# Two-block transformer kernel: the odd layer's first projection with another order of its block products, later reads of PSUM and another order of its loads

## The chip, the cores and the metric

The kernel runs on one core of one Trainium2 chip. The metric is the time of one execution of the whole program on the device, in microseconds. The program has two blocks: a transformer block with gated linear attention, differential attention and a feed-forward part, and a second block of two layers. The change touches the last third of the second block alone, its odd layer.

## What is computed, as far as it matters here

The odd layer normalizes and modulates x (1024 tokens of 1024 channels) to h, multiplies h by `odd_w_in` (1024 x 3072), mixes the columns with a pooling and a short convolution, and multiplies by `odd_w_out`; the result is added to x.

```python
def odd_mixer(h, w_in, w_out, p_w, p_scale, conv_w):
    p = h @ w_in
    ...
    y_c = pool_mix(p[..., :o1], p_w, p_scale)
    c_gate, x_path, b_gate, z = p[..., o1:o2], p[..., o2:o3], p[..., o3:o4], p[..., o4:]
    y_d = b_gate * short_conv(c_gate * x_path, conv_w)
    y = jnp.concatenate([y_c, y_d], axis=-1) * jax.nn.silu(z)
    return y @ w_out
```

## The kernel before

**Precision.** Operands of a product are held as a high and a low part (`hi`, `lo`), and every product of a 128x128 weight block with 512 columns of activations is three matmuls: hi by hi, hi by lo, lo by hi. For weights ScalarE (ACT) copies the high part and GpSimd (POOL) subtracts for the low part; `split_part` does so for weights that come through the ring of the helper `pump` (`raw` tiles, loaded on SP's queue at L183).

**Seven products for eight.** The 24 column blocks of `odd_w_in` are taken in 12 pairs p (the table `ODD`). For a pair, the weights are four quarters a11, a12, a21, a22 (128 x 512 numbers each), and h is four quarters too: two halves of the channels, by tokens 0 to 511 and 512 to 1023. A scheme of Strassen and Winograd's makes the 2 x 2 block product out of 7 products m = 1 to 7, each of 4 blocks k, so 12 matmuls. The activation sides (`ops[m]`, "forms") are made once, in `differences`: m = 1 and 2 take the tokens 0 to 511 of h, which are there first; 5, 6, 7, 3 and 4 need the second half normalized (`normed`) and then sums and differences of both halves (t1, t2 and so on), each split into a high part on ACT and a low part. The weight sides (`ODD_W`) are quarters or the sums s1 to s4, formed on VectorE (DVE) by `quarter_sum` in place, split by `halves` in `weight_steps`. Six buffers hold the quarters; `quarter` loads one on SP's queue, `free` gives one back.

**Order.** `ODD_ORDER` lists the products (m, p). Pairs 0 and 1 were interleaved at the start, so that their products with the first half of h come first and the forms are made under them; from p = 2 on the order is 1, 6, 2, 7, 5, 4, 3. `weight_steps` gives each weight step a due time in products; `prepare(n + 3)` in the loop does what is due three products ahead.

**PSUM places.** A product fills one bank of 512 columns. Two products in a row share one tile of two banks (`halves` in `product`), a "place" here; three places are used in turn. `evac(p)` reads finished products in the order of the list `order[p]`: m = 1 is copied by ACT, the others are added by DVE to the running sums t0 (`v`) and t1 (`y`). Before the change it was called after every product:

```python
            if n > 1:
                evac(p)
            step()
```

`step` runs one piece of the work that follows a pair (`after`): for p < 4 the pooling, with two small products `ps_w` (L2000) in PE's queue, for p from 4 on the convolution and the gate.

**The end.** `odd_w_out` comes through `pump` again; x, which had been stored to HBM, is loaded back (`x<-x_d`, 4 MB in 4 transfers, L2074) before the last residual, whose first products are `ps_x` (L220). In the last pair the finished columns are split for that product (`y_split`), in pieces between the products. Almost all instructions are issued through one helper and show its line, L65 (L68 after the change); so they are told apart by the tiles' names.

## Time and profile before

| | |
|---|---|
| median of 3 runs | 2405.98 us (2405.83 to 2413.56) |
| the profiled execution's own time | 2409.9 us |
| its span in the trace | 2408.1 us, so 1.8 us lie around it |
| busy: PE / DVE / POOL / ACT | 91% / 67% / 45% / 36% |
| mean granted clock of TensorE | 0.962 of full speed |
| the odd layer's first projection, 84 products | about 1981 to 2308 us |
| what follows it (residual, final norm) | 2308 to 2408 us |

A row of the timeline has the start, the length, the engine and line, the operation with its output and inputs by name, a count, and in brackets the time that the engine stood idle before it with what ended that. Matmuls overlap, so their pitch is read from starts, not from lengths.

### The profile page before, as it was taken

How to read it: one execution, taken by the hardware profiler on the slowest of the kernel's cores; microseconds unless marked ns; L12 is line 12 of the kernel's file. 1: busy time of each engine (PE TensorE's matmuls, PEld its weight loads, DVE VectorE, ACT ScalarE, POOL GpSimd, SP SyncE). 2: the span in 40 equal slices, each digit the busy share in tenths (PEclk: the TensorE clock that was granted, in tenths of full speed). 3: DMA queues.
4: the chain of work that ended last, by engine and by line, in shares of the span. 5: the costliest groups of instructions: out<-in, count | busy, mean ns of one | idle time of the engine just before them, and what ended most of it. 6: DMA issues, size and time to landing. Idle time of an engine off the chain costs nothing. (4 is left out here: it accounts for less than half of the span.)

```text
span 2408.1 us, 28852 instructions
## 1 busy us (share of the span) xinstructions
PE 2181.5 (91%) x10024; PEld 1763.0 (73%) x10024; DVE 1618.0 (67%) x2642; ACT 861.4 (36%) x1432; POOL 1092.4 (45%) x843
## 2 busy tenths in 40 slices
PE   6999998899999999989999997988879985888888
PEld 3777777688878888878787875877767774666666
DVE  8665656688366866798777657689875567554534
ACT  4324331588443222222232344422224433222333
POOL 7333332498433322223556425555443536453543
PEclk8999899999999999999999999998989998999999
DMA  7355664985423445212333333654526531121143
GB/s 266 109 170 192 209 210 151 270 236 174 164 90 108 146 134 181 85 59 91 108 105 114 112 90 108 181 174 147 175 97 222 180 105 49 45 66 44 47 158 114
DMA packets 191402, 330.41 MB, mean 137 GB/s; under 512 B 47330, under 2 KB 88194, under 8 KB 190996
## 3 DMA queue, kind: packets, MB, share of 16 engines
q1 hardware_dynamic: 190960, 328.34, 42.3%
q8 instruction: 79, 1.29, 0.2%
q14 instruction: 71, 0.58, 0.1%
q10 hardware_dynamic: 292, 0.20, 0.0%
HBM read 264.90 MB, written 67.46 MB: 138 GB/s over the span
## 5 line engine op out<-in xcount | busy, mean ns | idle before, releaser
L65 POOL TENSOR_TENSOR lo<-raw,hi 128x512 fp32r<-128x512 f32 (+3 forms) x414 | 509.5, 1244 | 762.4 <-ACT hi L65 502.1
L65 ACT ACTIVATE hi<-raw 128x512 fp32r<-128x512 f32 (+3 forms) x418 | 217.9, 549 | 387.2 <-PE ps_g L220 143.1
L220 PE MATMUL ps_g<-h0hi,hi 128*128 128x512 f32 x552 | 222.4, 403 | 12.7 <-ACT h0hi L65 8.0
L220 PE MATMUL ps_g<-h0lo,hi 128*128 128x512 f32 x552 | 218.7, 396 | 5.7 <-POOL h0lo L65 5.7
L220 PE MATMUL ps_g<-h1lo,hi 128*128 128x512 f32 x552 | 216.6, 392 | 5.9 <-DVE h1lo L65 5.9
L220 PE MATMUL ps_g<-h0hi,lo 128*128 128x512 f32 x552 | 218.7, 396 | 1.9 <-DVE lo L65 1.4
L220 PE MATMUL ps_g<-h1hi,hi 128*128 128x512 f32 x552 | 220.4, 399 | 0.0
L220 PE MATMUL ps_g<-h1hi,lo 128*128 128x512 f32 x552 | 216.3, 392 | 0.0
L65 DVE SCALAR_TENSOR_TENSOR u<-ps_g,vecs,u 128x1023 f32<-128x1023 f32 (+3 forms) x94 | 114.1, 1214 | 92.5 <-ACT u L65 89.7
L65 POOL TENSOR_TENSOR lo<-a,hi 128x512 fp32r<-128x512 f32 x80 | 114.8, 1461 | 130.9 <-ACT hi L65 94.3
L220 PEld LDWEIGHTS ps_g<-h0hi,hi 128*128 128x128 f32 x552 | 105.4, 191 | 38.9 <-ACT h0hi L65 9.2
L220 PEld LDWEIGHTS ps_g<-h0lo,hi 128*128 128x128 f32 x552 | 105.4, 191 | 28.5 <-POOL h0lo L65 7.0
L220 PEld LDWEIGHTS ps_g<-h1lo,hi 128*128 128x128 f32 x552 | 104.6, 189 | 29.0 <-DVE h1lo L65 7.2
L220 PEld LDWEIGHTS ps_g<-h0hi,lo 128*128 128x128 f32 x552 | 105.5, 191 | 25.2 <-DVE lo L65 1.8
L1934 PE MATMUL ps_o<-t,hi 128*128 128x512 f32 x288 | 95.1, 412 | 31.6 <-ACT hi L65 18.7
L220 PEld LDWEIGHTS ps_g<-h1hi,hi 128*128 128x128 f32 x552 | 104.7, 190 | 24.4 <-issue 2.2
L220 PEld LDWEIGHTS ps_g<-h1hi,lo 128*128 128x128 f32 x552 | 104.5, 189 | 22.3
L220 PE MATMUL ps_d<-acthi,hi 128*128 128x512 f32 x272 | 109.4, 402 | 11.9 <-DVE u L65 8.9
L220 PE MATMUL ps_d<-actlo,hi 128*128 128x512 f32 x272 | 108.1, 397 | 0.0
L220 PE MATMUL ps_d<-acthi,lo 128*128 128x512 f32 x272 | 107.5, 395 | 0.0
L65 DVE TENSOR_TENSOR acc<-acc,sq 128x512 f32<-128x512 f32 x69 | 73.9, 1072 | 47.0 <-ACT sq L65 46.0
L65 ACT ACTIVATE hi<-a 128x512 fp32r<-128x512 f32 x80 | 45.7, 621 | 150.6 <-DVE a L65 148.3
(445 smaller groups left out, 5611.9 us busy)
## 6 DMA issues: line engine op xcount, KB each, us to landing
adw<-in_ada_w_dram SPq DMA_DIRECT2D x48, 512.0 KB, 3.5
raw<-in_w_up_dram SPq DMA_DIRECT2D x88, 256.0 KB, 3.0
adw<-in_w_ada_dram SPq DMA_DIRECT2D x32, 512.0 KB, 5.7
bias<-bias_d SPq DMA_DIRECT2D x32, 512.0 KB, 4.6
a<-in_odd_w_in_dram SPq DMA_DIRECT2D x60, 256.0 KB, 3.0
raw<-in_w_in_dram SPq DMA_DIRECT2D x50, 256.0 KB, 3.9
raw<-in_even_w_in_dram SPq DMA_DIRECT2D x44, 256.0 KB, 3.5
raw<-in_w_down_dram SPq DMA_DIRECT2D x72, 128.0 KB, 2.7
```

The costliest lines, as they stand in the source:

```text
L65: return f(*a, **k)
L220: self.PE.matmul(out, lhsT=a[:, k], rhs=b, start=first and n == 0, stop=last and n == 2)
L1934: PE.matmul(out, lhsT=a[:, k], rhs=b[k], start=k + n == 0, stop=k == 3 and n == 2)
```

## The change

Pair 0 is multiplied as eight plain block products, with weights that come whole through `pump` (columns 0 and 16 of `odd_w_in`; one more weight in `seq`), and two of its products accumulate into the bank of an earlier one: (3,0) on (5,0) and (4,0) on (6,0). So there are 85 products in place of 84. The order of the first 22 products is written out anew, and from p = 3 on it is 1, 2, 6, 7, 5, 4, 3. `evac` is called only when both products of a place are issued. All forms are split on VectorE instead of GpSimd, after all normalized quarters are made first. The weight sums s2 and s4 are formed right behind each other, and the quarter a12 is loaded earlier in the order. The reload of x is issued after the loop, so behind eight transfers of `odd_w_out`.

```diff
-ODD_ORDER = [(m, p) for m in (1, 2, 5, 6, 7, 3, 4) for p in range(2)] + [(m, p) for p in range(2, 12) for m in (1, 6, 2, 7, 5, 4, 3)]
+
+ODD_ORDER = [(1, 1), (2, 1), (1, 0), (8, 0), (2, 0), (9, 0), (5, 0), (6, 0), (5, 1), (3, 0), (4, 0), (3, 1), (6, 1), (7, 1),
+             (1, 2), (2, 2), (6, 2), (4, 1), (7, 2), (5, 2), (4, 2), (3, 2)]
+ODD_ORDER += [(m, p) for p in range(3, 12) for m in (1, 2, 6, 7, 5, 4, 3)]
...
-        self.seq += [(I["odd_w_in"][n], 8) for n in range(2)]
+        self.seq += [(I["odd_w_in"][n], 8) for n in (1, 0, 16)]
...
-                self.quarter_sum(p, "s1", "a21", "a22", "a22", ALU.add)
-                yield
-                self.quarter_sum(p, "s3", "a11", "a21", "a21")
-                yield
-                self.quarter_sum(p, "s2", "s1", "a11", "a11")
+            for out, x, y, place, op in (("s1", "a21", "a22", "a22", ALU.add), ("s3", "a11", "a21", "a21", ALU.subtract),
+                                         ("s2", "s1", "a11", "a11", ALU.subtract), ("s4", "a12", "s2", "a12", ALU.subtract)):
+                self.quarter_sum(1, out, x, y, place, op)
...
-        t12, t22, t1, t2 = [], [], [], []
+        t12 = [normed(place(7, 1, k, F32), k) for k in range(4)]
+        t22 = [normed(place(4, 1, k, F32), 4 + k) for k in range(4)]
+        yield
+        t1, t2 = self.temps, []
         for k in range(4):
-            t12.append(normed(place(7, 1, k, F32), k))
-            t1.append(temp())
             V.tensor_tensor(out=t1[k], in0=t12[k], in1=t11[k], op=ALU.subtract)
-            split(G, 5, t1[k], k)
+            split(V, 5, t1[k], k)
             yield
         for k in range(4):
-            t22.append(normed(place(4, 1, k, F32), 4 + k))
+            A.activation(out=ops[3][0][k], in_=t22[k], func=ACTF.Identity, bias=shift(k))
             t2.append(place(4, 0, k, F32))
             V.scalar_tensor_tensor(out=t2[k], in0=t22[k], scalar=shift(k), in1=t1[k], op0=ALU.add, op1=ALU.subtract)
-            split(G, 6, t2[k], k)
+            V.scalar_tensor_tensor(out=ops[3][1][k], in0=t22[k], scalar=shift(k), in1=f(ops[3][0][k]), op0=ALU.add, op1=ALU.subtract)
+            yield
+        for k in range(4):
+            split(V, 6, t2[k], k)
             yield
         for k in range(4):
             t = self.temps[k]
             V.scalar_tensor_tensor(out=t, in0=t22[k], scalar=self.dsh[:, k:k + 1], in1=t12[k], op0=ALU.add, op1=ALU.subtract)
-            split(G if k < 3 else V, 7, t, k)
+            split(V, 7, t, k)
             yield
-        for k in range(4):
-            A.activation(out=ops[3][0][k], in_=t22[k], func=ACTF.Identity, bias=shift(k))
-            V.scalar_tensor_tensor(out=ops[3][1][k], in0=t22[k], scalar=shift(k), in1=f(ops[3][0][k]), op0=ALU.add, op1=ALU.subtract)
         for k in range(4):
             t = self.temps[k]
             V.tensor_tensor(out=t, in0=f(ops[2][0][k]), in1=t2[k], op=ALU.subtract)
             V.tensor_tensor(out=t, in0=t, in1=f(ops[2][1][k]), op=ALU.add)
-            split(G, 4, t, k)
+            split(V, 4, t, k)
...
-            if m in (3, 4, 5, 7):
+            if m > 2:
                 self.free(p, ODD_W[m])
 
         def last(p):
             self.quarter_sum(p, "s4", "a12", "s2", "a12")
-            self.free(p, "s2")
-
-        for p in range(12):
+
+        for p in range(1, 12):
             at = lambda m: ODD_AT[m, p]
             for m in range(1 if p > 1 else 3, 8):
                 add(at(m), 0, halves, m, p)
@@ -1888,10 +1884,9 @@
                     add(at(1) - 3, 1, self.quarter, p, name)
                 add(at(1) + 0.1, 0, self.quarter_sum, p, "s1", "a21", "a22", "a22", ALU.add)
                 add(at(1) + 0.2, 0, self.quarter_sum, p, "s3", "a11", "a21", "a21")
-                add(at(6) - 0.5, 0, self.quarter_sum, p, "s2", "s1", "a11", "a11")
-            q = at(2) if p > 1 else at(7)
-            add(q - 2, 1, self.quarter, p, "a12")
-            add(q + 1, 0, last, p)
+                add(at(2) + 0.5, 0, self.quarter_sum, p, "s2", "s1", "a11", "a11")
+                add(at(2) - 2, 1, self.quarter, p, "a12")
+                add(at(2) + 0.6, 0, last, p)
...
-            if m == 2 and p < 2:
-                out = self.pst.tile([128, 512], F32, tag="t", name="ps_2")
+            again = p == 0 and m in (3, 4)
+            if again:
+                out = banks[m + 2, 0]
             elif halves:
...
-                if m < 3 and p < 2:
-                    self.product(self.odd0 + p, out, k + 4 * (m - 1), rh[k], rl[k], k == 0, k == 3)
+                if p == 0:
+                    self.product(self.odd0 + 1 + (m in (8, 9, 6, 4)), out, k + 4 * (m in (2, 9, 3, 4)), rh[k], rl[k],
+                                 k == 0 and not again, k == 3 and m not in (5, 6))
+                elif p == 1 and m < 3:
+                    self.product(self.odd0, out, k + 4 * (m - 1), rh[k], rl[k], k == 0, k == 3)
...
-                        while len(todo) > 1:
-                            step()
+                    while len(todo) > 1:
+                        step()
                     t0[p] = first(p)
-                    A.activation(out=t0[p][:, H[0]], in_=ps, func=ACTF.Copy)
+                if m in (1, 8):
+                    A.activation(out=(second(p) if m == 8 else t0[p])[:, H[1]], in_=ps, func=ACTF.Copy)
                     continue
                 u = [t[:, h] for t in (t0[p], second(p)) for h in H]
-                for out, x in {6: ((1, 0),), 2: ((0, 0),), 7: ((2, 1),), 5: ((3, 2), (1, 1)), 4: ((2, 2),), 3: ((1, 1),)}[m]:
+                how = {2: ((0, 1),), 6: ((1, 1),), 7: ((2, 1),), 5: ((3, 2), (1, 1)), 4: ((2, 2),), 3: ((1, 1),), 9: ((2, 3),)}
+                if p == 0:
+                    how[4] = (3, 3),
+                for out, x in how[m]:
...
+            if m == 4 and p == 0:
+                self.release(self.odd0 + 1)
+                self.release(self.odd0 + 2)
+            elif m == 2 and p == 1:
+                self.release(self.odd0)
+            elif p > 1 or p == 1 and m > 2:
...
-            prepare(n if n < 4 else n + 3)
+            prepare(n + (5 if p == 11 else 3))
...
-                evac(0)
-                evac(1)
-                self.temps = [t[:, h] for t in wide for h in H]
...
-            if n > 1:
-                evac(p)
+                self.temps = [t[:, h] for t in wide for h in H]
+            if not halves or (m, p) == (3, 11):
+                for q in range(max(p - 1, 0), p + 1):
+                    evac(q)
...
-                for a in range(2):
-                    for k in (0, 4):
-                        S.dma_start(out=self.x[:, k:k + 4, H[a]], in_=self.x_d[:, k:k + 4, H[a]])
             if not steps:
                 self.n_max = len(self.seq)
                 self.pump()
-        i = self.odd0 + 2
+        while todo:
+            step()
+        for a in range(2):
+            for k in (0, 4):
+                S.dma_start(out=self.x[:, k:k + 4, H[a]], in_=self.x_d[:, k:k + 4, H[a]])
+        i = self.odd0 + 3
```

**ACT, from the forms t7 to the last weight of pair 1.** `t70`, `t40` and `h1hi` are high parts of forms, `hi<-a...` those of weights; `a21_27663` holds the weight sum s3 of pair 1, for the product (7,1). Before:

```order
L65 ACTIVATE t70_28525<-y6_28491 128x512
L65 ACTIVATE t70_28530<-y6_28491 128x512
L65 ACTIVATE t70_28535<-y7_28492 128x512
L65 ACTIVATE t70_28540<-y7_28492 128x512
L65 ACTIVATE hi_28546<-a11_27673 128x512
L65 ACTIVATE h1hi_18152<-t41f_28449,m21_17426 128x512
L65 ACTIVATE h1hi_18152<-t41f_28457,m21_17426 128x512
L65 ACTIVATE h1hi_18152<-t41f_28465,m21_17426 128x512
L65 ACTIVATE h1hi_18152<-t41f_28473,m21_17426 128x512
L65 ACTIVATE t40_28575<-y6_28491 128x512
L65 ACTIVATE t40_28581<-y6_28491 128x512
L65 ACTIVATE t40_28587<-y7_28492 128x512
L65 ACTIVATE t40_28593<-y7_28492 128x512
L65 ACTIVATE hi_28597<-a21_27663 128x512
```

Now:

```order
L68 ACTIVATE t60_28576<-t40f_28530 128x512
L68 ACTIVATE t70_28593<-y6_28433 128x512
L68 ACTIVATE t70_28598<-y6_28433 128x512
L68 ACTIVATE hi_28602<-a12_27669 128x512
L68 ACTIVATE t70_28626<-y7_28434 128x512
L68 ACTIVATE t70_28631<-y7_28434 128x512
L68 ACTIVATE hi_28635<-a11_27667 128x512
L68 ACTIVATE t40_28653<-y6_28433 128x512
L68 ACTIVATE t40_28659<-y6_28433 128x512
L68 ACTIVATE t40_28677<-y7_28434 128x512
L68 ACTIVATE t40_28683<-y7_28434 128x512
L68 ACTIVATE hi_28687<-a21_27663 128x512
```

The weight for (7,1) stands behind the four forms t40 in both; the h1hi rows (form 3) have gone to an earlier place, and two weights stand between the forms.

**DVE, in the middle of the layer, one pair each.** `v` and `y` with a `ps_o` input are reads of products, `a` rows are weight sums. Before:

```order
L65 TENSOR_TENSOR y3_28496<-ps_o_29028,y3_28496 128x512
L65 TENSOR_TENSOR v_28974<-ps_o_29028,v_28974 128x512
L65 TENSOR_TENSOR a22_28987<-a21_28985,a22_28987 128x512
L65 TENSOR_TENSOR a21_28985<-a11_28983,a21_28985 128x512
L65 TENSOR_TENSOR a11_28983<-a22_28987,a11_28983 128x512
L65 TENSOR_TENSOR y3_28496<-ps_o_29075,y3_28496 128x512
L65 TENSOR_TENSOR v_28974<-ps_o_29075,v_28974 128x512
L65 TENSOR_TENSOR a12_29052<-a12_29052,a11_28983 128x512
```

Now:

```order
L68 TENSOR_TENSOR v_29287<-ps_o_29295,v_29287 128x512
L68 TENSOR_TENSOR y4_28439<-ps_o_29295,v_29287 128x512
L68 TENSOR_TENSOR a22_29273<-a21_29271,a22_29273 128x512
L68 TENSOR_TENSOR a21_29271<-a11_29269,a21_29271 128x512
L68 TENSOR_TENSOR y4_28439<-ps_o_29332,y4_28439 128x512
L68 TENSOR_TENSOR v_29287<-ps_o_29332,v_29287 128x512
L68 TENSOR_TENSOR y4_28439<-ps_o_29332,y4_28439 128x512
L68 TENSOR_TENSOR a11_29269<-a22_29273,a11_29269 128x512
L68 TENSOR_TENSOR a12_29312<-a12_29312,a11_29269 128x512
```

Before, the three sums of the next pair (s1, s3, s2) stood in front of a read of the next product's place; now s1 and s3 stand behind the reads of one whole place and s2 and s4 behind those of the next.

**SP, the end of the odd layer.** `a` rows are the last quarters of weights, `raw` rows transfers of `odd_w_out`. Before:

```order
L1723 DMA a12_30059<-in_odd_w_in_dram 128x512
L1723 DMA a22_30121<-in_odd_w_in_dram 128x512
L2074 DMA x_30213<-x_d_125 128x4x512 x4
L183 DMA raw_30218<-in_odd_w_out_dram 128x512
L183 DMA raw_30220<-in_odd_w_out_dram 128x512
L183 DMA raw_30222<-in_odd_w_out_dram 128x512
L183 DMA raw_30224<-in_odd_w_out_dram 128x512
```

Now:

```order
L1722 DMA a12_30024<-in_odd_w_in_dram 128x512
L1722 DMA a22_30104<-in_odd_w_in_dram 128x512
L186 DMA raw_30164<-in_odd_w_out_dram 128x512
L186 DMA raw_30166<-in_odd_w_out_dram 128x512
L186 DMA raw_30168<-in_odd_w_out_dram 128x512
L186 DMA raw_30170<-in_odd_w_out_dram 128x512
L186 DMA raw_30233<-in_odd_w_out_dram 128x512
L186 DMA raw_30235<-in_odd_w_out_dram 128x512
L186 DMA raw_30288<-in_odd_w_out_dram 128x512
L186 DMA raw_30290<-in_odd_w_out_dram 128x512
L2082 DMA x_30207<-x_d_125 128x4x512 x4
L186 DMA raw_30358<-in_odd_w_out_dram 128x512
```

The reload of x stood in front of all transfers of `odd_w_out`, and stands behind eight of them now.

## Rows read from the trace of the kernel before

**Rows 1.** Windows: length, busy PE, PEld, DVE, ACT, POOL (count), clock, DMA.
```profile
1980.00:2055.00 75.00, 47.72 (x177) 35.54 (x176) 53.55 (x55) 25.29 (x41) 44.14 (x33) 0.84 0.13 43
...
2020.00:2030.00 10.00, 1.92 (x5) 1.56 (x6) 9.86 (x10) 3.89 (x7) 8.20 (x6) 0.50 0.01 2
...
2055.00:2292.00 237.00, 203.37 (x843) 155.34 (x841) 123.25 (x154) 56.44 (x94) 110.80 (x79) 1.00 0.18 58
```
**Rows 2.** Timeline, PE, pairs 6 and 7: start, length, instruction, idle before and releaser.
```profile
2144.33 0.39 PE L1934 MATMUL ps_o<-h1lo,hi 128*128 128x512 f32 x1
...
2149.32 0.39 PE L1934 MATMUL ps_o<-t,lo 128*128 128x512 f32 x1
...
2151.24 0.47 PE L1934 MATMUL ps_o<-h1hi,hi 128*128 128x512 f32 x1 [1.53 <-ACT hi L65]
...
2198.44 0.47 PE L1934 MATMUL ps_o<-h1hi,hi 128*128 128x512 f32 x1 [1.53 <-ACT hi L65]
```
**Rows 3.** Timeline, DVE, at the gap that ends at 2151.24.
```profile
2148.23 2.26 DVE L65 TENSOR_TENSOR a<-a,a 128x512 f32<-128x512 f32 x3
2150.41 0.68 DVE L65 TENSOR_TENSOR y<-ps_o,y 128x512 f32<-128x512 f32 x1
```
**Rows 4.** Timeline, PE, the first 14 products: the long waits and the product after them.
```profile
1983.33 1.12 PE L405 MATMUL ps_r<-acc,ones 128*128 128x512 f32 x2 [1.55 <-DVE acc L65]
...
2028.08 1.19 PE L1934 MATMUL ps_o<-t,hi 128*128 128x512 f32 x2 [13.69 <-ACT hi L65]
...
2054.56 0.39 PE L1934 MATMUL ps_o<-h0hi,hi 128*128 128x512 f32 x1
```
**Rows 5.** Timeline, DVE, ACT and POOL, while the forms are made.
```profile
1985.87 0.75 DVE L65 SCALAR_TENSOR_TENSOR t71f<-x,s,rs 128x512 f32<-128x512 f32 x1 [2.53 <-ACT rs L65]
...
2000.19 1.78 DVE L65 SCALAR_TENSOR_TENSOR t41f<-x,s,rs 128x512 f32<-128x512 f32 x1
...
1999.68 3.43 POOL L65 TENSOR_TENSOR t<-t40f,t 128x512 fp32r<-128x512 f32 x2
...
2025.74 0.63 ACT L65 ACTIVATE t<-y 128x512 fp32r<-128x512 f32 x1 [0.70 <-DVE y L65]
2026.28 1.72 ACT L65 ACTIVATE hi<-a 128x512 fp32r<-128x512 f32 x3
```
**Rows 6.** Groups of instructions, 2055 to 2292: line, engine, shape, count, busy and mean ns, idle before.
```profile
L65 POOL TENSOR_TENSOR lo<-a,hi 128x512 fp32r<-128x512 f32 x68 | 97.5, 1460 | 116.7 <-ACT hi L65 80.1 <-PE ps_o L1934 26.0 <-issue 9.8
L65 ACT ACTIVATE hi<-a 128x512 fp32r<-128x512 f32 x66 | 37.3, 621 | 130.0 <-DVE a L65 130.0
L65 DVE TENSOR_TENSOR v<-ps_o,v 128x512 f32<-128x512 f32 x39 | 26.8, 688 | 52.6 <-PE ps_o L1934 49.2 <-ACT hi L65 3.4
L65 DVE TENSOR_TENSOR a<-a,a 128x512 f32<-128x512 f32 x37 | 25.4, 687 | 1.7
L2000 PE MATMUL ps_w<-y,pw 128*128 128x512 f32 x16 | 7.7, 603 | 2.6 <-DVE y L65 1.4 <-issue 1.2
L65 DVE SCALAR_TENSOR_TENSOR y<-y,v 128x1024 f32<-128x1024 f32 x4 | 6.9, 1714 | 0.1
```
**Rows 7.** Timeline, PE, ACT, SP and DVE, at the layer's end.
```profile
2303.59 0.77 PE L1934 MATMUL ps_o<-h1hi,hi 128*128 128x512 f32 x1 [11.86 <-DVE y L65]
...
2308.01 0.39 PE L220 MATMUL ps_x<-h0hi,hi 128*128 128x512 f32 x1
...
2298.59 1.27 ACT L65 ACTIVATE hi<-raw 128x512 fp32r<-128x512 f32 x2 [15.29 <-DMA raw<-in_odd_w_out_dram]
...
2284.86 2.52 SPq L2074 DMA_DIRECT2D x<-x_d  x4
2287.48 37.18 SPq L183 DMA_DIRECT2D raw<-in_odd_w_out_dram  x14
...
2317.73 0.75 DVE L65 SCALAR_TENSOR_TENSOR x<-ps_x,m,x 128x512 f32<-128x512 f32 x1 [4.92 <-PE ps_x L220]
```
**Rows 8.** The page's table of DMA issues: the loads of weight quarters.
```profile
a<-in_odd_w_in_dram SPq DMA_DIRECT2D x60, 256.0 KB, 3.0
```

More of the change, by code (lines that the diff above doesn't have):

```diff
@@ L1413, in second_block @@
             self.release(i)
-            self.n_max = self.odd0 + 2
+            self.n_max = self.odd0 + 3
             self.pump()
@@ L1680, in even_out @@
         self.dsh = tp.tile([128, 64], F32, name="dsh")[:, 0:4]
-        for p in range(2):
-            for name in ("a21", "a22", "a11"):
-                self.quarter(p, name)
+        for name in ("a21", "a22", "a11", "a12"):
+            self.quarter(1, name)
         ns = ExitStack()
@@ L1699, in first_sums @@
         def first_sums():
-            for p in range(2):
-                self.quarter_sum(p, "s1", "a21", "a22", "a22", ALU.add)
-                yield
-                self.quarter_sum(p, "s3", "a11", "a21", "a21")
-                yield
-                self.quarter_sum(p, "s2", "s1", "a11", "a11")
+            for out, x, y, place, op in (("s1", "a21", "a22", "a22", ALU.add), ("s3", "a11", "a21", "a21", ALU.subtract),
+                                         ("s2", "s1", "a11", "a11", ALU.subtract), ("s4", "a12", "s2", "a12", ALU.subtract)):
+                self.quarter_sum(1, out, x, y, place, op)
                 yield
@@ L1742, in differences @@
         yield
-        def temp():
-            return tmp.tile([128, 512], F32, tag="nm", name="nm")
         def split(eng, m, src, k):
@@ L1905, in odd_layer @@
         banks, halves, turn, t0, vs, todo, late = {}, [], [2], {}, {}, deque(), []
-        order = [[1, 6, 2, 7, 5, 3, 4] if p < 2 else [1, 6, 2, 7, 5, 4, 3] for p in range(12)]
+        order = [[1, 8, 2, 9, 3, 4], [1, 2, 6, 7, 5, 3, 4]] + [[1, 2, 6, 7, 5, 4, 3] for p in range(2, 12)]
         P = 8
@@ L1926, in product @@
             banks[m, p] = out
-            rh, rl = ops[m]
+            rh, rl = ops[{8: 1, 9: 2, 6: 5, 4: 3}.get(m, m) if p == 0 else m]
             for k in range(4):
-                if m < 3 and p < 2:
-                    self.product(self.odd0 + p, out, k + 4 * (m - 1), rh[k], rl[k], k == 0, k == 3)
+                if p == 0:
[3 more added lines that the diff above has]
+                    self.product(self.odd0, out, k + 4 * (m - 1), rh[k], rl[k], k == 0, k == 3)
                 else:
@@ L1935, in product @@
                 yield
-            if m == 2 and p < 2:
-                self.release(self.odd0 + p)
-            elif m > 2 or p > 1:
+            if m == 4 and p == 0:
[4 more added lines that the diff above has]
+            elif p > 1 or p == 1 and m > 2:
                 del self.odd_split[m, p]
@@ L1947, in evac @@
                 if m == 1:
-                    if p > 1:
-                        while len(todo) > 1:
-                            step()
+                    while len(todo) > 1:
+                        step()
                     t0[p] = first(p)
-                    A.activation(out=t0[p][:, H[0]], in_=ps, func=ACTF.Copy)
+                if m in (1, 8):
+                    A.activation(out=(second(p) if m == 8 else t0[p])[:, H[1]], in_=ps, func=ACTF.Copy)
                     continue
                 u = [t[:, h] for t in (t0[p], second(p)) for h in H]
-                for out, x in {6: ((1, 0),), 2: ((0, 0),), 7: ((2, 1),), 5: ((3, 2), (1, 1)), 4: ((2, 2),), 3: ((1, 1),)}[m]:
+                how = {2: ((0, 1),), 6: ((1, 1),), 7: ((2, 1),), 5: ((3, 2), (1, 1)), 4: ((2, 2),), 3: ((1, 1),), 9: ((2, 3),)}
+                if p == 0:
+                    how[4] = (3, 3),
+                for out, x in how[m]:
                     V.tensor_tensor(out=u[out], in0=ps, in1=u[x], op=ALU.add)
@@ L2035, in y_split @@
                 eng.tensor_tensor(out=y(k, 1, h), in0=y32[k][:, H[h]], in1=y(k, 0, h).bitcast(F32), op=ALU.subtract)
+        self.pump()
         for n, (m, p) in enumerate(ODD_ORDER):
-            prepare(n if n < 4 else n + 3)
+            prepare(n + (5 if p == 11 else 3))
             for j, _ in enumerate(product(m, p)):
@@ L2041, in odd_layer @@
                     next(side)
-            if n < 4:
-                for _ in range(4):
-                    next(side)
-                prepare(n + 5)
-            if n == 1:
+            for _ in range(1 if n == 0 else 2):
+                next(side, None)
+            if n == 0:
                 ns.close()
```

## The prediction

> **What bounds the kernel now.** I read the table of windows first. In the odd layer's projection PE is busy for 47.7 of 75 us at the start, and for 203.4 of 237 us in the middle, at full clock there; VectorE is busy for 123 of those 237 us and GpSimd for 111 [rows 1]. So PE is nearest to a bound, and no other engine is full. Then the timeline of PE: from the 2nd matmul of a product pair to its last, 22 pitches, are 4.99 us, so 0.227 us for a matmul and 2.72 us for a product [rows 2]. The projection runs from 1981 to 2308.0 (the table of the profile, [rows 7]), 327 us, and its 84 products need 84 x 2.72 = 228.5. Some 98 us are waits or slow clock. They fall into three parts.
>
> - *Start.* The first 14 products end where the 15th begins, at 2054.56. The longest wait among them is one of 13.69 us for a high part from ACT [rows 4]; it stands behind forms that VectorE makes. At 2025.74 ACT copies the last form, and right behind it, at 2026.28, the weights for which PE waits [rows 5].
> - *Middle.* In the timeline every second product starts late. Two pairs of columns, 14 products, take 2198.44 - 2151.24 = 47.2 us [rows 2] instead of 38.1: seven places, 1.3 us each. At one of these gaps VectorE does three weight sums from 2148.23, and only then, at 2150.41, the read that lets PE go [rows 3]. The second product of a place waits until the first one has been read, because the read of one half and the write of the other count as the same tile.
> - *End.* The last product waits 11.86 us, to 2303.59 [rows 7]. The chain behind it is the order on ACT: the high part of `odd_w_out` starts at 2298.59 after 15.29 us of waiting for its transfer. That was issued at 2287.48, behind the 4 MB of x issued at 2284.86; ACT's next forms, VectorE's next low parts and the read of the place stand behind it.
>
> **The change, part by part.** I place each part against the profiled execution, 2409.9 us, of which the span is 2408.1.
>
> *One product more*: 2.72 us on PE. It stands in the term for the start, since 14 products stand ahead of (1,2) both times and 71 instead of 70 from there on.
>
> *Start.* The new order puts six products on the first half of h first: 6 x 2.72 from 1983.7, just behind the row sums at 1983.33 [rows 4], to 2000. VectorE meanwhile does eight normalized quarters from 1985.87 at 0.78 us (an estimate from the 0.75 us of one [rows 5]), to 1992.1. A form that VectorE splits itself is a serial chain: 0.69, ACT 0.62, 0.69 [rows 6] and hand-overs, 2.1 us as I take it; four of t1 go to 2001 with a read between. So (5,0), (6,0) and (5,1) find theirs with little wait, and (3,0), (4,0) need no new weights: to 2013.7. Eight operations for t2 and form 3 end at about 2007.4, four low parts and two reads at 2012, four t7 forms at 2.15 us at 2021, four t4 forms, with two more sums each, at 2.8 us at 2032. The next weights stand between these on ACT, so (3,1) and (6,1) wait about 2 us each and end at 2023. The weight of (7,1) stands behind the last t4 form, as the order on ACT shows, so it comes at about 2032. PE idles about 9 us there. In the wait of 13.69 us [rows 4] the granted clock was at half, 0.50 from 2020 to 2030 [rows 1], so I let (7,1) run its 12 matmuls at half speed, to 2038. Then the two small pooling products of pair 0 wait for GpSimd and VectorE, and (1,2) starts at 2041 instead of 2054.6. Gain 13.5, less the extra product: **10.8 us**. Most of it comes from the first waits; the long one only moves.
>
> What GpSimd loses here is not on PE's path; what VectorE gains is. When GpSimd works beside it, an operation of VectorE on 128 x 512 takes 1.78 us [rows 5] instead of 0.75. That is my bound for the worse: GpSimd still splits about seven weights in this stretch, 1.46 us each [rows 6], so some 10 us, in which seven operations can lose 1 us each. With none of them the start is 3 us better, with all of them and a slower weight 4 us worse; I take the middle, since half of them fall where VectorE waits for ACT. The Trainium skill (GPSIMD Engine Reference, Specifications) says that GpSimd shares its SBUF interfaces with VectorE, with contention for VectorE's instructions with two SBUF inputs. By that rule every split that the change moves to VectorE is exposed, which would put the start near the worse end, some 2352 us in all. It bears on the reads of PSUM the other way, as these have one SBUF input only; the trace agrees, as 39 reads average 0.688 us [rows 6] while GpSimd is busy almost half of the time.
>
> *Middle.* From 2054.56 to 2291.73 (2303.59 - 11.86) there are 237.2 us for 69 products (187.7): 49.5 us beside them. Of these 7.7 are the pooling products of four pairs [rows 6], and 41.8 are waits, the gaps of 1.3 us above all. The change reads a place only after both its products are done. Then the next wait for a place is for the one three turns back: two places, 4 x 2.72 = 10.9 us, lie between, and its reads need three or four times 0.61 us. So this wait goes altogether. What is late next are the weights. The sum s2 stands behind the reads of a place; from the start of the product after that place it takes 3 reads (1.9 us), the sum (0.69), ACT (0.62) and GpSimd (1.46) [rows 6], 4.7 us and with one long pooling operation (1.71) 6.4. The weight is needed three products later, 8.2 us. It is in time, but not by much. In the pooling pairs p = 1 to 3 PE itself stands still: the small products stand in its queue behind three reads, an edge product and 1.71 us on VectorE, which is 4.6 us after the product that they follow started, so 1.9 us late each. I take 6 us of waits in all (0 to 12), and 5.8 for the pooling products of these three pairs (the fourth stands in the start). Gain 49.5 - 5.8 - 6: **37.7 us**.
>
> *End.* From 2291.73 to 2308.01 are 16.3 us for one product, so 13.6 are lost. Now eight transfers of `odd_w_out` go ahead of x, so ACT has its weights before the last products. **13.6 us** gained, if x is not late instead. Its 4 MB took about 11 us of the queues in the trace (from 2287.5 to 2298.6, what the weights waited [rows 7]); it is issued some 5 us before the last product ends, and the first addition to x stands 9.7 us after that (2317.73 - 2308.01 [rows 7]). So its first half is there in time; the bounds are 0 and 4 us, I take 0.
>
> The deeper splitting of due times, two fewer sets of quarters and 2 more raw transfers cost nothing: SP's queue is idle, a quarter lands in 3.0 us [rows 8], and VectorE waited in all 1.7 us before its 37 weight sums [rows 6]. If that cover went, it would be the slower rival below.
>
> **Sum.** 10.8 + 37.7 + 13.6 = 62.1; 2409.9 - 62.1 = **2347.8, so 2348 us**. The median of the runs shown is 3.9 below the profiled execution; the range takes that in. The forecast's own range is 2334 (no waits in the middle, a start 4 us better, 3.9 for the median) to 2360.
>
> **Rivals.**
>
> *A. Weights take the place of the PSUM waits.* If the operations in the chain of s2 meet GpSimd and run at 1.78, and GpSimd's own queue has another low part ahead, the chain is 1.9 + 1.78 + 1.78 + 0.62 + 2 x 1.73 = 9.5, and with the pooling or convolution operation 11.2, so 3 us too late in each of ten pairs: 30 instead of the 6, 2372. For it: 66 high parts wait for VectorE's sums already [rows 6]. Against: these sums average 0.687 us, so they seldom meet GpSimd.
>
> *B. The start gives nothing.* VectorE does all forms alone, in series with ACT; if the contention above goes on for longer, the last t4 form comes near 2043 and the long wait eats the 10.8: 2359.
>
> *C. Slower than before.* Weight sums now stand between reads on VectorE, in order. If a sum waits for the load of its quarter (a buffer comes free only when GpSimd has split its former contents, which waits for PE), the reads behind it, and the next weights, wait too. The price per pair is a load of 3.0, two sums at 1.78, ACT 0.62 and GpSimd 1.73: 8.9 us. Ten pairs: 89 instead of 6, so 2431. It makes the kernel slower than before from about 7.5 us per pair. Against it: the six buffers are as many as before and the sums wait for almost nothing now.
>
> *D. The change does not do what it says:* the gaps stay, for another dependence between the halves of a place; only start and end gain, 24.4 us: 2385.
>
> **Chances.** Forecast 0.58, A 0.19, B 0.10, D 0.06, C 0.04, and 0.03 that gains and losses cancel. A measurement of this kernel can tell about 0.3%, 7.2 us, from no change. Faster by over that: 0.58 + 0.19 + 0.10 + 0.06 = 0.93; within it 0.03; slower 0.04. The range goes from 2334 to 2376: it holds the forecast, A and B, and leaves out D, C and no change (0.13) and a little below.
>
> **What would show it right or wrong.** In PE's timeline of the changed kernel: no idle before every second product in the middle, periods of 14 products near 38 us; one long wait for ACT at (7,1), near 2023 to 2032, with a lower clock behind it; (1,2) near 2041; no wait over 2 us before the last product. Waits `<-ACT hi` or `<-POOL lo` every seven products would be A, a sum that waits for a transfer C. Form operations of VectorE at 1.7 us throughout the start would be B. A first addition to x that waits for a transfer would show that the end is not wholly won.

## The result, and the profile after

The changed kernel takes 2349.86 us (median of 4 runs, 2344.56 to 2352.03) against 2408.77 us for the kernel before (4 runs): a ratio of 0.975, 95% interval 0.9724 to 0.9777. The profiled execution took 2352.03 us, with a span of 2350.3. Forecast were 2348 us, with a range of 2334 to 2376.

First the windows of the changed kernel: start and length, busy time and instructions of PE, weight loads, DVE, ACT and POOL, then granted clock, DMA share and rate.

```profile
2020.00:2030.00 10.00, 2.50 (x10) 1.74 (x10) 6.87 (x11) 3.04 (x6) 0.00 (x0) 0.76 0.10 26
2030.00:2040.00 10.00, 7.52 (x15) 4.47 (x16) 8.03 (x11) 3.41 (x7) 7.22 (x5) 0.67 0.09 26
...
2150.00:2200.00 50.00, 50.00 (x222) 41.42 (x221) 29.64 (x35) 16.02 (x26) 28.62 (x20) 1.00 0.26 79
...
2240.00:2260.00 20.00, 16.68 (x60) 12.54 (x59) 13.04 (x15) 7.21 (x12) 13.93 (x10) 0.83 0.73 250
```

In the window from the middle, 2150 to 2200, PE is never idle; before the change it was busy for 203.4 of 237 us [rows 1]. It still loses time at the start (2020 to 2040) and, which is new, behind the layer (2240 to 2260). PE's timeline names the waits, from the first product to the residual:

```profile
1979.11 0.39 PE L223 MATMUL ps_o<-h0hi,hi 128*128 128x512 f32 x1
...
2030.06 1.22 PE L1933 MATMUL ps_o<-t,hi 128*128 128x512 f32 x2 [7.55 <-ACT hi L68]
...
2038.16 2.99 PE L2005 MATMUL ps_w<-y,pw 128*128 128x512 f32 x4 [2.29 <-issue]
2040.16 1.42 PE L1933 MATMUL ps_o<-h0hi,hi 128*128 128x512 f32 x1
...
2243.13 0.39 PE L223 MATMUL ps_x<-h0hi,hi 128*128 128x512 f32 x1
...
2250.04 0.50 PE L223 MATMUL ps_x<-h0hi,hi 128*128 128x512 f32 x1 [1.87 <-ACT hi L68]
2251.78 0.79 PE L223 MATMUL ps_x<-h0hi,lo 128*128 128x512 f32 x1 [0.94 <-POOL lo L68]
```

The first addition to x, on VectorE, waits for PE:

```profile
2259.72 0.75 DVE L68 SCALAR_TENSOR_TENSOR x<-ps_x,m,x 128x512 f32<-128x512 f32 x1 [5.20 <-PE ps_x L223]
```

Between 2041 and 2238 all of PE's waits are these (line, releaser, total us, times, longest):

```profile
PE ps_w L2005 <- DVE y L68: 2.3, 3, 0.8
```

That is 2.3 us in three waits, one for each pooling pair that is left in the middle; the gaps before every second product [rows 2] and the wait of 11.86 us before the last one [rows 7] are gone.

The 57.8 us between the two spans add up so. The layer begins 1.8 us earlier (1979.1 for 1980.9), which is well inside what this start varies by, as said below, so I don't put it down to the change. The first 14 products take 61.1 us (1979.11 to 2040.16) in place of 73.6, but 71 and not 70 follow: 12.6 - 2.7 = 9.9 gained. From there to the first residual product it was 253.45 us for 70 products and is 202.97 for 71; beside the products 62.9 and 9.7, so 53.2 gained. From the first residual product to the first addition to x it was 9.72 [rows 7] and is 16.59 (2243.13 to 2259.72): 6.9 lost. The rest of the program differs by 0.2.

In the experiments I use one length beside the median: from the layer's first product to the first addition to x, 336.8 us before and 280.6 in the changed kernel. The layer itself begins anywhere from 1970.4 to 1980.9 us in the profiled executions of nearly the same program, and medians of few runs carry that; this length doesn't. It comes from one profiled execution of each kernel.

### The profile page after: what moved, and what is told of

Read it like the earlier page. It is cut to its first block, busy times and chain, and to the rows that moved or that the text cites. A ratio compares the mean times of both kernels' runs of the same rounds, so it can differ in the third digit from the quotient of the medians.

```text
span 2350.3 us, 28842 instructions
## 1 busy us (share of the span) xinstructions
PE 2181.1 (93%) x10036; PEld 1768.6 (75%) x10036; DVE 1614.9 (69%) x2650; ACT 861.3 (37%) x1430; POOL 1065.9 (45%) x825
## 5 line engine op out<-in xcount | busy, mean ns | idle before, releaser
L1933 PE MATMUL ps_o<-t,hi 128*128 128x512 f32 x264 | 83.4, 397 | 8.8 <-ACT hi L68 8.8
L68 DVE TENSOR_TENSOR t<-ps_i,rot 64x480 f32<-64x480 f32 (+3 forms) x108 | 64.8, 600 | 34.9 <-PE ps_i L1512 28.4
```

Of the source, the lines that this page charges most:

```text
L68: return f(*a, **k)
L1933: PE.matmul(out, lhsT=a[:, k], rhs=b[k], start=k + n == 0, stop=k == 3 and n == 2)
```

## The experiments

| run | median us | ratio to before, 95% | length, us | up to the residual | from there (granted clock) |
|---|---|---|---|---|---|
| before | 2408.77 | | 336.8 | 327.1 | 9.7 (1.00) |
| the change | 2349.86 | 0.9724 to 0.9777 | 280.6 | 264.0 | 16.6 (0.79) |
| r1 read after every product | 2399.25 | 0.9939 to 0.9971 | 327.5 | 317.4 | 10.1 (1.00) |
| r2 before, reads in pairs alone | 2372.16 | 0.983 to 0.9892 | 302.5 | 283.5 | 19.0 (0.77) |
| r3 x ahead | 2349.23 | 0.9731 to 0.9786 | 280.5 | 263.9 | 16.6 (0.79) |
| r4 residual's weights ahead | 2341.47 | 0.9702 to 0.9757 | 277.4 | 264.0 | 13.5 (1.00) |
| r5 the end as before | 2352.36 | 0.974 to 0.9797 | 288.4 | 270.5 | 17.9 (0.71) |
| r6 low parts of forms on GpSimd | 2343.30 | 0.9699 to 0.9769 | 276.6 | 261.4 | 15.3 (1.00) |
| r7 weight ahead of forms | 2345.74 | 0.9723 to 0.9772 | 278.3 | 262.7 | 15.6 (0.89) |
| r8 r4 and r7 | 2346.63 | 0.9703 to 0.9766 | 277.0 | 262.6 | 14.4 (0.88) |
| r9 low parts one form behind | 2335.54 | 0.9668 to 0.9725 | 269.6 | 254.3 | 15.3 (1.00) |
| r10 r4 and r9 | 2331.52 | 0.9662 to 0.9713 | 268.0 | 254.6 | 13.5 (1.00) |
| r11 r10 and a block on VectorE | 2336.23 | 0.9678 to 0.9736 | 268.3 | 254.4 | 13.9 (1.00) |

Each ratio is taken against runs of the kernel before on the same chip. The length is given in two parts as well, up to the residual's first product and from there, because the granted clock of the second part is not the same in all runs. In the changed kernel it is 0.79, and the matmuls from 2251.78 to 2257.45 go 0.43 us apart, the level of 1.2 GHz. In r9 PE waits there for nearly the same (0.50, 1.85, 1.00 and 0.68 us in place of 0.51, 1.87 and 0.94), but the clock is 1.00 and the matmuls go 0.23 us apart. The windows of the second part, of the changed kernel,

```profile
2243.13:2259.72 16.59, 13.27 (x44) 9.73 (x43) 9.63 (x13) 6.93 (x12) 10.80 (x8) 0.79 0.88 302
```

and of r9 and r4:

```profile
2232.05:2247.30 15.25, 11.19 (x44) 7.68 (x43) 9.62 (x13) 6.94 (x12) 10.79 (x8) 1.00 0.90 323
2234.31:2247.79 13.48, 11.00 (x47) 8.48 (x46) 11.78 (x13) 5.12 (x9) 10.82 (x7) 1.00 0.86 292
```

So some 1.3 us of this part, 16.59 for 15.25, go with the clock. What made it fall in one run and not in the other is not shown.

### Reads in pairs: r1 takes them out, r2 puts them in alone

```diff
-            if not halves or (m, p) == (3, 11):
+            if True:
                 for q in range(max(p - 1, 0), p + 1):
                     evac(q)
```

> The changed kernel, but a product is read as soon as it is issued and not only when its PSUM place holds both. Theory G (the gaps of the middle are the wait of a place's second product for the read of its first): every second product is late again by 1.2 to 1.5 us, some 35 places, so 35 to 50 us more than the changed kernel, 2385 to 2400 us, with PE idle for VectorE's or ACT's reads before every second product. Rival O (the new order and the earlier weights give the gain of the middle): at most 10 us more, 2350 to 2360 us, and no such idle time.

The run lost 46.9 us of length (49.4 by the medians): 5.4 up to the product (1,2), 48.0 from there to the residual, and 6.5 came back in the residual's start. So nearly all of the 53.2 us that the change gained in the middle and at the end goes again. The waits of its PE from 1975 to 2320, the five largest groups: line, releaser, total us, times, longest.

```profile
PE ps_o L1933 <- DVE v L68: 19.2, 16, 2.8
PE ps_o L223 <- DVE v L68: 9.7, 2, 7.4
PE ps_o L1933 <- ACT v L68: 8.6, 6, 2.5
PE ps_o L223 <- ACT v L68: 8.3, 2, 7.1
PE ps_o L1933 <- DVE y L68: 7.9, 9, 0.9
```

Nearly all are waits for reads of PSUM (`v` and `y`), as theory G has it. Two of more than 7 us stand at the start: there a place's first half is read behind the forms.

Alone on the kernel before:

```diff
-            if n > 1:
-                evac(p)
+            if n > 1 and (not halves or (m, p) == (3, 11)):
+                for q in range(max(p - 1, 0), p + 1):
+                    evac(q)
```

> The kernel before with one part of the change alone: products are read only when their PSUM place holds both; order, forms, weights and loads as before. Theory G: the gaps of the middle go, 30 to 42 us less than before, 2366 to 2379 us, with the start (15th product near 2054 us) and the wait before the last product (about 12 us) as before. Rival O: less than 10 us gained, and waits for weights, ACT or GpSimd, in place of the gaps, since the sums are due as late as before.

It gained 34.3 us of length: 1.7 up to the 15th product, 41.8 from there to the residual, and 9.3 were lost behind that. Behind the pooling pairs the middle is without a wait here too, with the old order and the old due times of the sums (a window of the middle):

```profile
2110.00:2230.00 120.00, 120.00 (x531) 99.37 (x530) 78.42 (x88) 34.78 (x57) 66.70 (x45) 1.00 0.20 64
```

One thing I had not expected: the wait before the last product went with it and came back in the residual, since the last product's place no longer stands behind that read.

```profile
2254.26 0.80 PE L220 MATMUL ps_x<-h0hi,hi 128*128 128x512 f32 x1 [3.81 <-ACT hi L65]
...
2265.92 0.47 PE L220 MATMUL ps_x<-h0hi,hi 128*128 128x512 f32 x1 [4.45 <-DVE v L65]
```

So the late reads are worth some 34 of the 56 us by themselves. Of rival O nothing is left in the middle: the new order and the earlier weights don't close the gaps, since r1 has both and has the gaps.

### The end: r3 and r5

> The changed kernel, but with the reload of x issued behind the last pair's product 7 again, ahead of what is left of the transfers of odd_w_out. Theory E (the order of the two on the queue of transfers made the wait before the last product): a wait of 8 to 14 us comes back before the last product or in the first residual products, 2358 to 2364 us. Rival (part of odd_w_out is loaded before that point anyway, or reads in pairs leave more slack): within 3 us of the changed kernel.

```diff
             if p == 11 and m == 7:
                 self.sw2.close()
                 self.open_x()
+                for a in range(2):
+                    for k in (0, 4):
+                        S.dma_start(out=self.x[:, k:k + 4, H[a]], in_=self.x_d[:, k:k + 4, H[a]])
```

(and without these lines behind the loop). Nothing changed: 280.5 us. SP's queue shows why that was no test of the order:

```profile
2222.09 5.54 SPq L186 DMA_DIRECT2D raw<-in_odd_w_out_dram  x4
2232.93 2.35 SPq L2077 DMA_DIRECT2D x<-x_d  x4
```

The last pair's weights are due five products ahead now, so four transfers of `odd_w_out` had gone before x all the same. r5 takes that back as well (`prepare(n + 3)` throughout):

> The changed kernel with both parts of its end undone: x is reloaded behind the last pair's product 7, and the last pair's weights are due three products ahead and not five, so all of odd_w_out is issued behind x. (The run with x alone moved still had four of its transfers ahead of x.) Theory E (transfers of odd_w_out that stand behind x cost the end 8 to 13 us): the time from the layer's first product to the first addition to x grows by 8 to 13 us over the changed kernel's 280.6, 2357 to 2363 us. Rival P (reading in pairs took the last product out of the chain, so the late weights are covered): within 3 us of it.

The length is 7.8 us longer, just under what theory E named and clearly above the rival's 3. Its ACT waits for the transfer as before, and PE for ACT:

```profile
2242.96 1.32 ACT L68 ACTIVATE hi<-raw 128x512 fp32r<-128x512 f32 x2 [14.19 <-DMA raw<-in_odd_w_out_dram]
...
2243.64 0.50 PE L223 MATMUL ps_x<-h0hi,hi 128*128 128x512 f32 x1 [3.54 <-ACT hi L68]
```

So the first two weights have to be ahead of the 4 MB of x; it is the earlier due time that puts them there, and moving x behind the loop adds nothing to it. Not all of the 7.8 us is the transfer: PE also waits 0.60 and 1.61 us for low parts of the last pair's own weights, which stand behind the finished columns on GpSimd with the later due time, and the granted clock behind the layer is 0.71 in place of 0.79. The medians (2352.36 and 2349.86) would not have told the two apart.

### The residual's late start: r4

In the changed kernel the second weight of the residual stands on ACT behind the work on the last columns:

```profile
2244.88 0.63 ACT L68 ACTIVATE y<-y 128x512 f32<-128x512 f32 x1 [6.36 <-DVE y L68]
2247.80 1.67 ACT L68 ACTIVATE t<-y 128x512 fp32r<-128x512 f32 x3 [2.28 <-DVE y L68]
2249.37 0.61 ACT L68 ACTIVATE hi<-raw 128x512 fp32r<-128x512 f32 x1
```

ACT stands for 6.36 us in front of VectorE's read and then copies three column blocks, with this weight behind them and PE waiting at 2250.04. The edit calls the helper that splits these weights, `pump`, ahead of the reads:

```diff
+            if not steps:
+                self.n_max = len(self.seq)
+                self.pump()
             if not halves or (m, p) == (3, 11):
```

> The changed kernel, but in the last pair the weights of odd_w_out are split as soon as a product has given its ring space back, ahead of that product's reads and of the splits of the last columns. Theory W (the 6.9 us that the residual now loses at its start are weight splits that stand behind the last columns' work on ACT and GpSimd): the time from the first residual product to the first addition to x falls from 16.6 to 10 to 13 us, and the kernel gains 3 to 7 us, 2343 to 2347 us. Rival X (x or the transfers are late, or it is the clock alone): no gain, within 2 us of the changed kernel.

The length fell by 3.2 us to 277.4, and the residual's start from 16.6 to 13.5 us, just short of the 10 to 13 expected. PE's wait for ACT is gone, but not all of the 3.1 us is the order on ACT: r6 and r9, without this edit, have 15.3 us there at the full clock that r4 has too. So 1.8 us are left for the order, and 1.3 go with the clock; whether the edit keeps the clock up is not shown. Theory W holds for a smaller size than expected, and the clock that rival X names is a part. The 8.4 us between the medians are more than this stage can have given. What PE still waits for is the weight's low part on GpSimd:

```profile
2241.78 0.50 PE L223 MATMUL ps_x<-h0hi,lo 128*128 128x512 f32 x1 [1.96 <-POOL lo L68]
```

And the first addition now stands right behind VectorE's low part of the last columns, no longer behind PE:

```profile
2247.18 0.69 DVE L68 TENSOR_TENSOR t<-y,t 128x512 fp32r<-128x512 f32 x1 [0.70 <-ACT t L68]
2247.79 1.44 DVE L68 SCALAR_TENSOR_TENSOR x<-ps_x,m,x 128x512 f32<-128x512 f32 x2
```

### The start: r6, r7, r8

r6 turns `split(V, ...)` into `split(G, ...)` for the forms 5, 6, 7 and 4.

> The changed kernel with the low parts of the forms of products 5, 6, 7 and 4 on GpSimd again (16 operations, most of which GpSimd did before the change). Theory V (moving them to VectorE is part of the gain at the start): GpSimd takes 1.3 to 1.8 us for each, VectorE's operations beside them take 1.7 instead of 0.7, and the 15th product comes 5 to 15 us later, 2355 to 2365 us. Rival (GpSimd is idle there for 17 and 10 us at a stretch, and the chain through ACT and VectorE is what is long): within 3 us, or up to 6 us faster.

Theory V fell: the length is 276.6, 4.0 us shorter than with VectorE, 2.7 of it up to the residual and 1.3 behind it, at another granted clock. VectorE is slowed by GpSimd just as foreseen, but between two forms of product 7 or 4 it has nothing to wait for. VectorE's timeline of this run, forms of products 7 (a group of four) and 4:

```profile
2004.83 3.77 DVE L68 SCALAR_TENSOR_TENSOR y<-t41f,dsh,t71f 128x512 f32<-128x512 f32 x4
2008.52 1.76 DVE L68 TENSOR_TENSOR y<-h0hi,t40f 128x512 f32<-128x512 f32 x1
2010.32 1.63 DVE L68 TENSOR_TENSOR y<-y,h0lo 128x512 f32<-128x512 f32 x1
2011.88 1.78 DVE L68 TENSOR_TENSOR y<-h0hi,t40f 128x512 f32<-128x512 f32 x1
...
2022.04 0.68 DVE L68 TENSOR_TENSOR v<-ps_o,v 128x512 f32<-128x512 f32 x1
```

and of the changed kernel, the first form of product 7 and the last of product 4:

```profile
2008.85 0.74 DVE L68 SCALAR_TENSOR_TENSOR y<-t41f,dsh,t71f 128x512 f32<-128x512 f32 x1
2010.29 0.69 DVE L68 TENSOR_TENSOR t<-y,t 128x512 fp32r<-128x512 f32 x1 [0.70 <-ACT t L68]
...
2027.35 0.68 DVE L68 TENSOR_TENSOR y<-h0hi,t40f 128x512 f32<-128x512 f32 x1
2028.07 0.69 DVE L68 TENSOR_TENSOR y<-y,h0lo 128x512 f32<-128x512 f32 x1
2029.52 0.69 DVE L68 TENSOR_TENSOR t<-y,t 128x512 fp32r<-128x512 f32 x1 [0.76 <-ACT t L68]
```

Four forms of product 7 take 3.7 us of VectorE's time there (2004.83 to 2008.52), and here, with the low part and 0.70 us of waiting for ACT's copy in each, 9.2 (2008.85 to 2018.09). The forms of product 4, two sums each, are the longer ones there, 13.5 us for 12.0. Over all forms the stops and the operations that VectorE no longer has outweigh the slowing.

r7 issues the forms of product 4 only behind the split of the weight for (7,1), and the pooling of pair 0 three products later:

```diff
-            for _ in range(1 if n == 0 else 2):
+            for _ in range(1 if n == 0 else 2 if n < 9 or n > 10 else 0):
                 next(side, None)
...
-            step()
+            if n not in (10, 11, 12):
+                step()
```

> The changed kernel, but the four forms of product 4 are issued two products later, behind the split of the weight for product (7,1), and the pooling of pair 0 three products later. Theory S (the long wait of the start, 7.6 us, and the half clock behind it come from the order on ACT alone): no wait over 3 us before (7,1), the 15th product starts 5 to 10 us earlier, 2340 to 2345 us. Rival D (VectorE's own work, forms, reads and sums, is as long as that whatever the order): the wait moves to (1,2), (6,2) or (4,1), and less than 3 us are gained.

The wait before (7,1) went, and came back two products later in front of the pooling products, which need VectorE's forms, reads and sums done:

```profile
2037.76 3.70 PE L2005 MATMUL ps_w<-y,pw 128*128 128x512 f32 x4 [7.55 <-issue]
```

VectorE works from 2021.47 to 2037.66 without a stop of more than its 0.76 us for ACT, and its last pooling operation ends 0.1 us before these products. Only 2.3 us of length were gained, 1.4 of them up to the residual. Rival D holds: the order on ACT decides where PE waits, VectorE's work decides how long.

> The changed kernel with both: the weight of (7,1) ahead of the forms of product 4, and the weights of odd_w_out ahead of the last pair's reads and splits. If S and W both hold and do not meet: 8 to 13 us less than the changed kernel, 2337 to 2342 us, 267 to 273 us from the layer's first product to the first addition to x. If D holds: as the run with the weights of odd_w_out first alone, 277 us.

It measured 277.0 us, as D says for the two together. The parts of r7 and r4 don't add up to it (2.3 and 3.2 for 3.6), since both lengths hold a share of the clock behind the layer.

### VectorE's chain itself: r9, r10, r11

If VectorE's chain is the bound, its own idle time is what is to be had. In r9 VectorE computes the next form's source before the low part of the last:

```diff
+        def late_split(m, src, k):
...
+            A.activation(out=hi, in_=src, func=ACTF.Copy)
+            flush()
+            pend.append((lo, src, hi))
+
+        def flush():
+            while pend:
+                lo, src, hi = pend.pop()
+                V.tensor_tensor(out=lo, in0=src, in1=f(hi), op=ALU.subtract)
...
-            split(V, 5, t1[k], k)
+            late_split(5, t1[k], k)
```

(the same for 7 and 4, with a `flush` behind each t2 and behind the last form).

> The changed kernel, but VectorE computes the source of the next form before the low part of the last one (forms 5, 7 and 4), so that it doesn't stand for ACT's copy. Theory H (the start is set by VectorE's chain, in which each of 12 forms waits 0.70 to 0.76 us for ACT, 8.8 us in all, whoever makes the low part): the wait of 7.6 us before (7,1) falls to 0 to 2 us and the pooling products of pair 0 come 6 to 9 us earlier, 272 to 275 us from the layer's first product to the first addition to x against 280.6. Rival Q (the sums, reads and GpSimd's shift behind the forms are what PE waits for, as in the run with the weight ahead of the forms): under 3 us.

The length fell by 11.0 us to 269.6, below the 272 to 275 expected. VectorE goes through these forms without a stop for ACT but one of 0.15 us,

```profile
2014.60 0.69 DVE L68 TENSOR_TENSOR y<-h0hi,t40f 128x512 f32<-128x512 f32 x1
2015.32 0.69 DVE L68 TENSOR_TENSOR y<-y,h0lo 128x512 f32<-128x512 f32 x1
2015.93 0.69 DVE L68 TENSOR_TENSOR t<-y,t 128x512 fp32r<-128x512 f32 x1
2016.53 0.69 DVE L68 TENSOR_TENSOR y<-h0hi,t40f 128x512 f32<-128x512 f32 x1
```

and of PE's waits for ACT, 9.5 us in three, one of 3.0 us is left (0 to 2 expected):

```profile
PE ps_o L1949 <- ACT hi L68: 3.0, 1, 3.0
```

The waits before (3,1) and (6,1), 3.7 us in the changed kernel, are gone as well. Up to (1,2) the gain is 8.7 us, as much as VectorE's stops were (8.6 by their rows: four of 0.70, four of 0.70 and four of 0.76). So Theory H is shown. The rest of the 11.0 is the clock: 1.0 us in the product (1,2), which runs at a granted clock of 0.98 in place of 0.74, and 1.3 behind the residual's first product.

> The changed kernel with VectorE's low parts one form behind and the weights of odd_w_out ahead of the last pair's reads and splits. If H and W both hold: 269 to 272 us from the layer's first product to the first addition to x, 8 to 12 us less than the changed kernel as a whole, 2338 to 2342 us. If Q holds: as the run with the weights of odd_w_out first alone, 277 us.

268.0 us and a median of 2331.52: the lowest of both here, though the median's interval overlaps with those of r9 and r11. Against the changed kernel that is 12.6 us of length, a little more than the 8 to 12 expected, and 18 us by the medians, which is more than this stage gave; against the kernel before a ratio of 0.9687 (0.9662 to 0.9713). H and W add up where they don't share the clock: 9.4 us up to the residual, and behind it 1.8 for the order on top of the 1.3 that r9 has already.

> As the run before, and the low part of the last but two finished column block is made on VectorE instead of GpSimd. Theory L (what is left of the residual's late start, 1.96 us for a low part of a weight, stands on GpSimd behind that column block): the wait before the second residual weight goes, 1 to 3 us less than the run before. Rival (VectorE's reads of the last products then come later by 1.4 to 3.5 us, and with them the last columns): no gain or up to 3 us lost.

(`y_split(k + 1, V if k == 4 else G)`.) 268.3 us: no gain. The wait of 1.96 us for GpSimd went, and shorter ones for VectorE, ACT and GpSimd (0.17, 0.60 and 0.78 us) took its place, while the first addition came no earlier: it stands right behind VectorE's last low part (2238.49, then 2239.11), as in r4 and r10, and VectorE's reads of the last products came 3.2 us later than in r10, counted from the layer's first product. That is the rival.

## Why the prediction was right

**The start** was forecast to give 10.8 us and gave 9.9. The path was the one named: PE idle before (7,1) for ACT, whose copy stood behind the last form of product 4; I had put the wait at about 9 us and it was 7.6. (1,2) was put at 2041, and came at 2040.2 with the layer begun 1.8 us earlier. What sets its length is VectorE's chain of forms, as I had summed it, and not the order on ACT (r7). Where the 9.9 us come from is only in part shown: the late reads give 1.7 (r2) to 5.4 (r1) of them, the move of the splits to VectorE costs 1.9 up to (1,2) (r6), and for the rest, the new order of products with its plain pair 0, there is no run by itself. The granted clock was at 0.76 and 0.67 in the two windows from 2020 to 2040, and the matmuls of (7,1) went 0.43 us apart, which is the level of 1.2 GHz, as I had taken from [rows 1] and [rows 4].

**The middle and the end** were forecast to give 37.7 + 13.6 = 51.3 us and gave 53.2. I had allowed 6 us of waits, 1.9 for each pooling pair; these pairs waited 0.8, 0.7 and 0.8. At the first of them VectorE was done 3.6 us after the product began and not 4.6, as its pooling operation took 1.23 us and not 1.71. No weight was late, so A did not come about, though the sums did get longer (775 ns in the mean in place of the 687 of [rows 6]). That the end is a term beside the middle was only half right: r2 shows that reading in pairs alone takes the wait away from the last product and leaves it to the residual, and r5 that the earlier weights then save 7.8 us of it, not 13.6. In the sum that makes no difference, as the change has both. That transfers of `odd_w_out` have to be ahead of x was right (r5), but the due times put them there, and not the place of x behind the loop (r3). There is one set of quarters less than before (55 loads in place of 60), not two; nothing hangs on it.

**What I missed** is the 6.9 us at the residual's start. I looked at x there (bounds 0 and 4 us, 0 taken), and the first addition waited for PE, not for a transfer. That this term was 0 is partly luck: x was issued at 2244.60, 1.5 us behind the residual's first product and not 5 us before the last product's end, and landed 6.9 to 13.1 us later; an addition 9.7 us behind that first product would have come 8.2 us after the issue. The step that failed is that ACT "has its weights before the last products": that held for the first weight only; the second stood behind the last columns, which now end at the same time as the layer. Of the 6.9 us, 3.3 are waits for ACT and GpSimd (1.87, 0.51 and 0.94), and most of the rest are matmuls at half the clock behind them. r4 takes 3.1 back, 1.8 by the order and 1.3 with the clock, and 3.8 stay.

Like with like, the profiled execution of 2352.03 us, the forecast of 2347.8 was 4.2 us too low; the median is nearer to it because it lies 2.2 us below that execution. The terms were off by 0.9 (start), 1.9 the other way (middle and end) and 6.9 (residual), and the earlier layer took 1.8 off. So the total is better than its largest term, and that is luck.

**The weighed rule.** r6 shows VectorE at 1.63 to 1.86 us for 13 of its operations on forms while GpSimd works beside it, and its read of PSUM between them at 0.68 us. The Trainium skill (GPSIMD Engine Reference, Specifications) names the contention for instructions with two SBUF inputs, and the trace agrees. But what I drew from it, that moving the splits to VectorE exposes them and costs time near the worse end, was the wrong way to look: in the changed kernel GpSimd is idle for most of that stretch, so only 3 of VectorE's form operations were stretched to 1.6 or 1.8 us. The move cost 2.7 us up to the residual for another reason, VectorE's stops for ACT (r6, r9). I had counted those stops in the 2.1 us of a form, and not seen them as what could be had. B was this chance, and it did not happen.

C, D and a cancelling did not come about: no sum waited long for a transfer, and the gaps went.

## What to carry to other kernels

Where two results share one PSUM tile, reading the first before the second is written makes the writer wait once per tile; read both together if other tiles give the time for it (34 of 337 us here, r2). Before an operation is moved to a faster engine, look whether that engine's queue then alternates with another's: a lag of one step between source and low part gave back more (9.7 us up to the residual, r9) than the choice of engine (2.7, r6). And when a stage's waits are taken away, look at the first weights of the next stage: what was hidden under the old wait is now in front. And before a small difference in length is put down to an edit, compare the granted clock of the stretch in both runs.

## What the runs showed that I had not expected

That VectorE in the chain with ACT loses 0.70 to 0.76 us at each hand-over and back for a copy of 0.63 us, and that removing 12 of these gained as much as they add up to (8.7 us up to (1,2) for 8.6). That slowing VectorE's operations from 0.7 to 1.7 us, by giving work to GpSimd, can still be the faster choice (r6, 2.7 us up to the residual). And that the layer's start varies by some 10 us between executions while the length of the stage repeats closely: the run with x moved alone measured 280.5 against 280.6. And that nearly the same waits behind the layer are followed by a granted clock of 0.79 in one kernel and of 1.00 in another.
